# Transposing rows of q, k and the index query unsplit, two heads at once, and scoring each pair of heads on the two halves of the array's rows

## The chip, the cores and the metric

The kernel runs on one core of one Trainium2 chip. The metric is the device time of one execution in microseconds (us). Three runs of the kernel before took 591.34, 591.34 and 590.7 us, with a median of 591.34 us. The profile shown here belongs to one more execution, which took 590.16 us.

## The reference, cut to what matters

The program is one layer of a streaming encoder on 256 tokens of width 1024, in float32. An input projection yields, among other things, 16 query heads, 4 key and value heads, 8 heads of an index query with one shared index key (all of 64 elements), and the inputs of a state-space branch. The index scores choose 64 keys for every token, attention runs over the chosen keys, and the state-space branch runs beside it. Both branches are merged, and a mixture of 32 experts follows.

```
q  = rope(rmsnorm(q));  k = rope(rmsnorm(k));  iq = rope(iq);  ik = rope(rmsnorm(ik))
score[q,s]  = sum_h  iw[q,h] * relu(iq[q,h,:] . ik[s,:] / 8)         (8 index heads)
chosen[q]   = the 64 keys s with the largest score among the admissible ones
logit[h,q,s] = q[q,h,:] . k[s,h//4,:] / 8      for the chosen s      (16 heads)
o = softmax(logit) @ v
x = x + (sigmoid(ga) * (o @ W_a) + sigmoid(gb) * (ssd @ W_b)) @ W_out
x = x + experts(rmsnorm(x))
```

The part that the change touches is the way from the normalized rows of q, k, iq and ik to the two kinds of scores.

## The kernel before, in words

**Two parts per number.** Most matmuls run on operands of the type float32r, and a float32 value is kept as a rounded high part and a low part that holds the difference. A product of two such values takes three matmuls: high by high, high by low, low by high (`PASSES`). The weights come from memory as `w_raw` and are split into `w_hl`: ScalarE makes the high part (L174), and VectorE or GpSimd makes the low part (L178).

**Stages.** The tokens form two tiles of 128 (t = 0 and 1). The projections of q, k, the index query and the gates run as chunks of 512 columns (`wide_chunk`, L316), those of the state-space branch as chunks of 256 columns (`cm_chunk`, through `mm3`, L263). Beside these chunks runs a side stream, the generator `side()`, from which `interleave` takes a step between chunks: it handles the index key, the index query, the keys, the index scores, the queries and the attention. Later come the state-space groups, the branch projections (`ps_A`, `ps_S`), the output projection (`ps_o`), the routing, and eight rounds of four experts (`pgu`, `py`, `acc`) whose weights `we` stream in from memory on SyncE's queue, 96 tiles in a ring.

**The order of the work** is set by a planner, which simulates a timeline and gives each engine its list; each engine then goes through its list in order. Program order counts as priority, so a side step that is ready goes ahead of the chunk that follows it.

**From rows to scores.** `qk_tile` puts out the normalized and rotated rows `qn` of one token tile, 128 by heads by 64. `split_stack` (q and the index query, 8 heads at once) makes a tile `st` in which the high part (ScalarE, L389) and the low part (VectorE, L390) of each head lie side by side, 128 wide. `stack_T` transposes each head's 128 columns on TensorE against the identity (L379) and copies four heads at a time out of PSUM, on ScalarE (L382) for the first four, on VectorE (L384) for the others. So in `qT` and `iqT` a head's high part lies on partitions 0 to 63 and its low part on 64 to 127. `key_tile` does the same for keys, but stacks high on high and, in a second tile, low on low (L397, L399). A head's score then takes two matmuls over all 128 rows: the query's stack against the high keys, then against the low keys (L464 for the index, L541 in `attention`). 68 transposes, 32 matmuls of index scores and 64 of attention scores are issued in all.

**Buffers.** The pool `paux` in PSUM has two buffers with the tag "x" (transposes, `pt`, `po`) and two with the tag "s" (scores, a bank each). In `attention` one "s" buffer holds the scores of two heads; VectorE reads it with an instruction for each head (L545) that adds the bias and takes the maximum. In `index_proc` ScalarE reads it with one instruction (L467).

## Time and profile before

| quantity | value |
|---|---|
| median of three runs | 591.34 us |
| the profiled execution | 590.16 us |
| its span, from the first to the last instruction | 588.3 us |
| TensorE busy | 555.8 us, 94% of the span |
| VectorE busy | 332.1 us, 56% |
| ScalarE busy | 272.3 us, 46% |
| GpSimd busy | 240.0 us, 41% |
| memory read | 157.54 MB |

The busy share of TensorE is that of overlapping records: a matmul's record is longer than the time until the next one starts. The time that a run of equal matmuls takes is read from the start of the run to the start of the next one.

### The profile page before, as it was taken

The page shows a single profiled execution, that of the slowest core. Times are in us where ns is not written, and L with a number is a line of the kernel's source. Part 1 is how long each engine was busy: PE and PEld are TensorE (multiplying, and loading weights), DVE is VectorE, ACT ScalarE, POOL GpSimd, SP SyncE. Part 2 cuts the span into 40 slices and gives each one's busy share as a digit, 9 for nine tenths or more (in the row PEclk, how much of TensorE's full clock was granted, in tenths as well). Part 3 has the DMA queues.
Part 4 walks back from the last instruction along what each step waited for, and adds up shares of the span by engine and source line. Part 5 has one row for each costly group of instructions (what it writes and reads, how often), then busy time and mean ns, then how long its engine had stood idle before and what let it go on. Part 6 is the DMA issues. An engine that isn't in the chain of part 4 may idle for free.

```text
span 588.3 us, 9924 instructions
## 1 busy us (share of the span) xinstructions
PE 555.8 (94%) x3605; PEld 401.1 (68%) x3605; DVE 332.1 (56%) x711; ACT 272.3 (46%) x633; POOL 240.0 (41%) x250
## 2 busy tenths in 40 slices
PE   8999989999999999999999999999898898896996
PEld 5878768798898999889878888954354354241422
DVE  4669974999995888999594656551111212110101
ACT  7567567658897688877763535500000000000001
POOL 4677685666764376675767644100000000000000
PEclk9999999999999999999999999999999998987999
DMA  7755255353334595445766599989999999999994
GB/s 270 253 175 180 72 162 154 125 189 125 129 125 161 174 365 214 143 129 185 237 218 253 180 346 387 406 332 418 418 413 413 419 419 409 418 418 421 409 414 153
DMA packets 35811, 159.27 MB, mean 271 GB/s; under 512 B 4144, under 2 KB 5808, under 8 KB 27184
## 3 DMA queue, kind: packets, MB, share of 16 engines
q1 hardware_dynamic: 34464, 157.30, 71.2%
q10 hardware_dynamic: 1296, 1.30, 0.6%
q8 instruction: 30, 0.49, 0.3%
q14 instruction: 21, 0.17, 0.1%
HBM read 157.54 MB, written 1.05 MB: 270 GB/s over the span
## 4 chain that ended last, share of the span: by engine, by line
PE 63%; DMA 19%; DVE 8%; issue 3%; POOL 3%; ACT 2%; SPq 0%; ACTq 0%; DVEq 0%; POOLq 0%
DMA we<-wgu 13%; PE ps_xs L263 8%; PE ps_S L316 7%; PE ps_z L263 6%; PE ps_g L316 5%; PE pgu L1059 4%; DMA we<-wdn 4%; PE ps_A L316 4%; PE py L1119 3%; PE ps_g L1052 3%; PE acc L1134 2%; PE ps_o L316 2%; PE ps_k L316 2%; PE ps_iq L316 2%; PE ps_o L263 2%
## 5 line engine op out<-in xcount | busy, mean ns | idle before, releaser
L178 POOL TENSOR_TENSOR w_hl<-w_raw,w_hl 128x512 fp32r<-128x512 f32 (+1 forms) x101 | 140.7, 1396 | 87.8 <-ACT w_hl L174 70.1
L174 ACT CAST w_hl<-w_raw 128x512 fp32r<-128x512 f32 (+1 forms) x212 | 125.8, 620 | 47.7 <-PE ps_S L316 19.0
L178 DVE TENSOR_TENSOR w_hl<-w_raw,w_hl 128x512 fp32r<-128x512 f32 (+1 forms) x111 | 97.9, 889 | 36.6 <-ACT w_hl L174 36.0
L1059 PE MATMUL pgu<-we,xg 128*32 128x512 f32 x512 | 63.4, 603 | 4.6 <-DMA we<-wgu 4.6
L1077 POOL TENSOR_TENSOR dc<-Dm,cmr 128x128 f32<-128x128 f32 x16 | 6.1, 401 | 148.8 <-DVE Dm L982 133.5
L263 PE MATMUL ps_z<-hT,w_hl 128*128 128x256 f32 x384 | 51.6, 286 | 0.0
L263 PE MATMUL ps_xs<-hT,w_hl 128*128 128x256 f32 x384 | 50.7, 285 | 0.0
L263 PEld LDWEIGHTS ps_z<-hT,w_hl 128*128 128x128 f32 x384 | 47.7, 190 | 2.0 <-issue 1.8
L263 PEld LDWEIGHTS ps_xs<-hT,w_hl 128*128 128x128 f32 x384 | 47.5, 191 | 2.1 <-issue 2.1
L316 PE MATMUL ps_g<-w_hl,gT 128*128 128x512 f32 x192 | 47.8, 398 | 0.0
L316 PE MATMUL ps_S<-w_hl,yT 128*128 128x512 f32 x192 | 44.9, 392 | 0.0
L1055 DVE TENSOR_TENSOR xg<-ps_g,cmoe 128x512 f32<-128x512 f32 (+2 forms) x18 | 11.4, 631 | 56.8 <-PE ps_g L1052 56.7
L1059 PEld LDWEIGHTS pgu<-we,xg 128*32 128x32 f32 x512 | 15.4, 110 | 40.8 <-issue 25.9
L1052 PEld LDWEIGHTS ps_g<-Dm,x_sb 128*128 128x128 f32 x256 | 31.2, 191 | 16.5 <-issue 13.0
L316 PEld LDWEIGHTS ps_g<-w_hl,gT 128*128 128x128 f32 x192 | 35.1, 188 | 8.8 <-issue 0.8
L316 PEld LDWEIGHTS ps_S<-w_hl,yT 128*128 128x128 f32 x192 | 35.7, 188 | 7.6 <-issue 0.2
L1119 PE MATMUL py<-we,aTt 128*32 128x512 f32 (+1 forms) x272 | 35.7, 651 | 4.1 <-DVE aTt L1105 2.1
L1097 DVE SCALAR_TENSOR_TENSOR ac<-th,pgu 128x256 f32<-128x256 f32 x8 | 3.4, 421 | 60.6 <-ACT th L1095 60.6
L1130 ACT COPY y<-py 128x512 f32<-128x512 f32 (+1 forms) x9 | 4.8, 539 | 65.5 <-PE py L1119 65.5
L1052 PE MATMUL ps_g<-Dm,x_sb 128*128 128x128 f32 x256 | 33.5, 280 | 0.0
L1134 PE MATMUL acc<-y,dcT 128*128 128x512 f32 (+1 forms) x68 | 32.4, 604 | 0.9 <-DVE y L1132 0.8
L1095 ACT ACTIVATE th<-pgu,rs 128x256 f32<-128x256 f32 x8 | 3.8, 474 | 60.4 <-PE pgu L1059 60.4
(308 smaller groups left out, 977.0 us busy)
## 6 DMA issues: line engine op xcount, KB each, us to landing
we<-wgu SPq DMA_DIRECT2D x42, 1024.0 KB, 13.6
w_raw<-wwide SPq DMA_DIRECT2D x60, 512.0 KB, 3.7
we<-wdn SPq DMA_DIRECT2D x25, 1024.0 KB, 13.7
w_raw<-win SPq DMA_DIRECT2D x44, 512.0 KB, 3.8
we<-wgu SPq DMA_DIRECT2D x44, 512.0 KB, 10.3
we<-wdn SPq DMA_DIRECT2D x14, 512.0 KB, 10.2
x_sb<-xin SPq DMA_DIRECT2D x2, 512.0 KB, 4.4
w_raw<-wsm SPq DMA_DIRECT2D x1, 512.0 KB, 5.7
```

Source lines behind the costliest of these rows:

```text
L174: return act.copy(self.hl[i][:, 0], self.raw[i])
L178: return eng.tensor_sub(hl[:, 1], self.raw[i], hl[:, 0].bitcast(F32))
L263: pe.matmul(ps, lhsT=lhs[k][:, a], rhs=rhs[k][:, b], start=j == 0 and k == 0 and i == 0, stop=j == len(regions) - 1 and k == KD - 1 and i ...
L316: pe.matmul(ps[t], lhsT=lhs[t][k][:, a], rhs=w[k][:, b], start=k == 0 and i == 0, stop=k == KD - 1 and i == 2)
L1052: pe.matmul(ps[:, kk, :], lhsT=x1[:, t, (k + kk) * P:(k + kk + 1) * P], rhs=Dm[:, t].rearrange("p e j -> p (e j)"), start=t == 0, stop=t == 1)
L1055: dve.tensor_tensor(xg[:, ks, :], ps, fgain[:, ks].unsqueeze(2).to_broadcast([P, n, P]), op=ALU.mult)
L1059: i = pe.matmul(pgu[32 * e:32 * e + 32, :], lhsT=xg[:, k, 32 * e:32 * e + 32], rhs=wg[k][e], start=k == 0, stop=k == KD - 1, tile_position ...
L1077: pool.tensor_tensor(dc[:, t], Dm[:, t], cmr[:, t, 4 * q:4 * q + 4].unsqueeze(2).to_broadcast([P, 4, NSLOT]), op=ALU.mult)
L1095: act.activation(th, pgu[:, 0:256], AF.Tanh, scale=rs)
L1119: i_py = pe.matmul(py[32 * e:32 * e + 32, :], lhsT=aTt[:, f, 32 * e:32 * e + 32], rhs=wd[2 * n + f][e][:, c], start=f == 0, stop=f == 1, t ...
L1130: act.copy(y, py)
L1134: pe.matmul(acc[t][n][:, c], lhsT=dcT[:, t * P:(t + 1) * P], rhs=y, start=False, stop=q == 7 and c.stop == 512)
```

## The change

Four helpers are replaced. `heads_T` transposes the unsplit rows, two heads (128 columns) at once, so that one head of a pair lies on partitions 0 to 63 and the other on 64 to 127; the split into high and low part is made while the result is copied out of PSUM, by one instruction of ScalarE and one of VectorE. Keys and the index key are first doubled (`kd`, a copy on ScalarE) so that each key head lies on both halves. `pair_scores` then scores a pair of heads: three passes, and in each pass one matmul over rows 0 to 63 and one over rows 64 to 127, into two different "s" buffers. `index_proc` and `attention` take two "s" buffers at once, for four heads, where they took one at a time for two.

```
@@ -370,35 +370,27 @@
         pool.tensor_tensor(qn[:, :, 8:16], rc[:, :, 8:16], rs[:, :, 0:8], op=ALU.add)
         yield qn
 
-    def stack_T(dst, st, t, nh, name):
-
-        for h0 in range(0, nh, 4):
-            n = min(4, nh - h0)
-            ps = paux.tile([P, 4, P], F32, tag="x", name="psT_" + name)
-            for h in range(n):
-                pe.transpose(ps[:, h, :], st[:, h0 + h].rearrange("p a d -> p (a d)").bitcast(F32), ident)
-            o = dst[:, h0:h0 + n, t * P:(t + 1) * P]
-            if h0 == 0:
-                act.copy(o, ps[:, :n, :])
-            else:
-                dve.tensor_copy(o, ps[:, :n, :])
-
-    def split_stack(dst, qn, t, nh, name):
-
-        st = att.tile([P, 8, 2, HD], F32R, tag="st", name="st_" + name)[:, :nh]
-        act.copy(st[:, :, 0, :], qn)
-        dve.tensor_sub(st[:, :, 1, :], qn, st[:, :, 0, :].bitcast(F32))
-        stack_T(dst, st, t, nh, name)
-
-    def key_tile(dst_hi, dst_lo, qn, t, nh, name):
-        st = att.tile([P, 8, 2, HD], F32R, tag="st", name="st_" + name)
-        sth, stl = st[:, 0:nh], st[:, 4:4 + nh]
-        for a in range(2):
-            act.copy(sth[:, :, a, :], qn)
-        for a in range(2):
-            dve.tensor_sub(stl[:, :, a, :], qn, sth[:, :, 0, :].bitcast(F32))
-        stack_T(dst_hi, sth, t, nh, name + "h")
-        stack_T(dst_lo, stl, t, nh, name + "l")
+    def heads_T(dst, qn, t, n, name, twice=False):
+
+
+        ps = paux.tile([P, 4, P], F32, tag="x", name="psT_" + name)
+        if twice:
+            kd = att.tile([P, 4, 2, HD], F32, tag="kd", bufs=1, name="kd_" + name)[:, :n]
+            act.copy(kd, qn.unsqueeze(2).to_broadcast([P, n, 2, HD]))
+            qn = kd.rearrange("p h a d -> p (h a) d")
+        for i in range(n):
+            pe.transpose(ps[:, i, :], qn[:, 2 * i:2 * i + 2].rearrange("p a d -> p (a d)"), ident)
+        o = dst[:, :, :n, t * P:(t + 1) * P]
+        act.copy(o[:, 0], ps[:, :n, :])
+        dve.tensor_sub(o[:, 1], ps[:, :n, :], o[:, 0].bitcast(F32))
+
+    def pair_scores(q, k, i, tok, nk, out):
+
+
+        for n, (a, b) in enumerate(PASSES):
+            for r in range(2):
+                rows = slice(HD * r, HD * r + HD)
+                pe.matmul(out[r], lhsT=q[rows, a, i, tok], rhs=k[rows, b, :nk], start=n == 0, stop=n == 2)
 
     def interleave(chunks, side, per):
 
@@ -422,8 +414,8 @@
 
     iws = att1.tile([P, 2, 8], F32, name="iws")
     dtx = ssd1.tile([P, 2, 32], F32, name="dtx")
-    ikT = att1.tile([P, 2, T], F32R, name="ikT")
-    iqT = bigt([P, 8, T], F32R, "iqT")
+    ikT = att1.tile([P, 2, 1, T], F32R, name="ikT")
+    iqT = bigt([P, 2, 4, T], F32R, "iqT")
     v_sb = att1.tile([P, 2, 256], F32, name="v_sb")
 
     def first_chunk():
@@ -444,10 +436,10 @@
         for t in range(2):
             q = qk_tile(ps0[:, t, 0:64], t, 1, 2, "ik")
             next(q)
-            key_tile(ikT[:, 0:1, :], ikT[:, 1:2, :], next(q), t, 1, "ik")
+            heads_T(ikT, next(q), t, 1, "ik", twice=True)
 
     def iq_proc(q, t):
-        split_stack(iqT, next(q), t, 8, "iq")
+        heads_T(iqT, next(q), t, 4, "iq")
 
     iq_scale = 0.125 * 8
 
@@ -456,22 +448,21 @@
     def index_proc(t):
         nk = P * (t + 1)
         sc = att1.tile([P, nk], F32, name=f"sc{t}")
-        for hp in range(4):
-            ps = paux.tile([P, 2, T], F32, tag="s", name="ps_i")
-            for hh in range(2):
-                h = 2 * hp + hh
+        tok = slice(t * P, (t + 1) * P)
+        for p0 in range(0, 4, 2):
+            ps = [paux.tile([P, 2, T], F32, tag="s", name="ps_i") for _ in range(2)]
+            for i in range(2):
+                pair_scores(iqT, ikT[:, :, 0], p0 + i, tok, nk, [ps[r][:, i, :nk] for r in range(2)])
+            for r in range(2):
+                rel = att.tile([P, 2, T], F32, tag="sm", bufs=SMB, name="rel")[:, :, :nk]
+                act.activation(rel, ps[r][:, :, :nk], AF.Relu, scale=iq_scale)
                 for i in range(2):
-                    pe.matmul(ps[:, hh, :nk], lhsT=iqT[:, h, t * P:(t + 1) * P], rhs=ikT[:, i, :nk],
-                              start=i == 0, stop=i == 1)
-            rel = att.tile([P, 2, T], F32, tag="sm", bufs=SMB, name="rel")[:, :, :nk]
-            act.activation(rel, ps[:, :, :nk], AF.Relu, scale=iq_scale)
-            for hh in range(2):
-                h = 2 * hp + hh
-                if h == 0:
-                    dve.tensor_scalar(sc, rel[:, 0, :], iws[:, t, 0:1], None, op0=ALU.mult)
-                else:
-                    dve.scalar_tensor_tensor(sc, rel[:, hh, :], iws[:, t, h:h + 1], sc, op0=ALU.mult, op1=ALU.add)
-            yield
+                    h = 2 * (p0 + i) + r
+                    if h == 0:
+                        dve.tensor_scalar(sc, rel[:, 0, :], iws[:, t, 0:1], None, op0=ALU.mult)
+                    else:
+                        dve.scalar_tensor_tensor(sc, rel[:, i, :], iws[:, t, h:h + 1], sc, op0=ALU.mult, op1=ALU.add)
+                yield
         dve.memset(sc[0:64, nk - 64:nk], NEGI)
         dump(f"sc{t}", sc)
         for r in range(8):
@@ -490,15 +481,15 @@
     def k_proc(ps, t):
         if t == 0:
             kT.append(bigt([P, 2, 4, T], F32R, "kT"))
-        key_tile(kT[0][:, 0], kT[0][:, 1], next(ps), t, 4, "k")
+        heads_T(kT[0], next(ps), t, 4, "k", twice=True)
 
     def v_proc(ps, t):
         act.activation(v_sb[:, t], ps[t][:, 256:512], AF.Copy, scale=rx[:, t:t + 1])
 
     def q_proc(ps, c, t):
         if t == 0:
-            qT.append(bigt([P, 8, T], F32R, f"qT{c}"))
-        split_stack(qT[c], next(ps), t, 8, f"q{c}")
+            qT.append(bigt([P, 2, 4, T], F32R, f"qT{c}"))
+        heads_T(qT[c], next(ps), t, 4, f"q{c}")
 
     def h_part(k2):
 
@@ -527,22 +518,21 @@
 
     def attention(t, jp):
         nk = P * (t + 1)
+        tok = slice(t * P, (t + 1) * P)
         PTs = []
         for jj in range(2):
             j = 2 * jp + jj
             PT = [att.tile([P, 4, P], F32, tag=f"PT{kt}", name=f"PT{kt}") for kt in range(t + 1)]
             PTs.append(PT)
+            ps = [paux.tile([P, 2, T], F32, tag="s", name="ps_s") for _ in range(2)]
             for g2 in range(2):
-                ps = paux.tile([P, 2, T], F32, tag="s", name="ps_s")
-                for gg in range(2):
-                    h = 4 * j + 2 * g2 + gg
-                    q = qT[h // 8][:, h % 8, t * P:(t + 1) * P]
-                    for i in range(2):
-                        pe.matmul(ps[:, gg, :nk], lhsT=q, rhs=kT[0][:, i, j, :nk], start=i == 0, stop=i == 1)
+                p = 2 * j + g2
+                pair_scores(qT[p // 4], kT[0][:, :, j], p % 4, tok, nk, [ps[r][:, g2, :nk] for r in range(2)])
+            for g2 in range(2):
                 sm = att.tile([P, 2, T], F32, tag="sm", bufs=SMB, name="sm")[:, :, :nk]
                 mx = att.tile([P, 2], F32, tag="mx", name="mx")
                 for gg in range(2):
-                    dve.tensor_tensor_reduce(out=sm[:, gg, :], in0=ps[:, gg, :nk], in1=bias_t[t], scale=1.0,
+                    dve.tensor_tensor_reduce(out=sm[:, gg, :], in0=ps[gg][:, g2, :nk], in1=bias_t[t], scale=1.0,
                                              scalar=SENT, op0=ALU.add, op1=ALU.max, accum_out=mx[:, gg:gg + 1])
                 act.activation(mx, mx, AF.Copy, scale=-8.0)
                 su = att.tile([P, 2], F32, tag="su", name="su")
@@ -570,7 +560,6 @@
             late = po_half(1, kt)
             with tc.issue_after(late.ins):
                 po_half(0, kt)
-        tok = slice(t * P, (t + 1) * P)
         act.copy(aT[jp][:, 0, :, tok], po)
         dve.tensor_sub(aT[jp][:, 1, :, tok], po, aT[jp][:, 0, :, tok].bitcast(F32))
```

## Rows read from the trace of the kernel before

**Rows 1.** Busy time by stretch: us, time and instructions of each engine, clock, DMA.
```profile
28.00:185.00 157.00, 153.17 (x948) 131.62 (x948) 130.60 (x297) 111.74 (x284) 106.32 (x116) 1.00 0.45 146
185.00:330.00 145.00, 144.80 (x1010) 126.20 (x1007) 118.09 (x210) 104.00 (x221) 89.30 (x75) 1.00 0.60 208
...
443.00:588.00 145.00, 122.87 (x808) 50.83 (x804) 22.27 (x49) 9.56 (x20) 3.04 (x8) 0.93 0.96 390
```

**Rows 2.** The chain that ended last: start us, us, what.
```profile
409.38 1.72 PE acc L1134 x4
...
454.73 19.88 DMA we<-wgu
```

**Rows 3.** What TensorE waited for between 28 and 180 us: total, times, longest.
```profile
PE ps_q L316 <- POOL w_hl L178: 2.0, 2, 1.0
PE ps_s L541 <- DVE mx L545: 1.7, 3, 0.8
```

**Rows 4.** GpSimd in order of time: start us, us, what, idle time before.
```profile
58.82 1.29 POOL L506 TENSOR_TENSOR h<-gT 128x512 f32<-128x512 f32 x1 [4.23 <-DVE sc L473]
64.71 0.25 POOL L99 TENSOR_SCALAR ss_q<-ss_q 128x8 f32<-128x8 f32 x1 [4.59 <-DVE ss_q L355]
...
78.31 1.72 POOL L178 TENSOR_TENSOR w_hl<-w_raw,w_hl 128x512 fp32r<-128x512 f32 x1
```

**Rows 5.** TensorE in order of time, transposes and scores before.
```profile
89.21 1.03 PE L379 MATMUL psT_q<-ident,st_q 128*128 128x128 f32 x8
90.00 1.09 PE L541 MATMUL ps_s<-kT,qT 128*128 128x128 f32 x8
90.93 1.15 PE L316 MATMUL ps_q<-w_hl,gT 128*128 128x512 f32 x4
...
113.55 0.87 PE L541 MATMUL ps_s<-kT,qT 128*128 128x256 f32 x6
114.25 5.77 PE L316 MATMUL ps_g<-w_hl,gT 128*128 128x512 f32 x24
```

**Rows 6.** TensorE in order of time, a run on two column halves.
```profile
151.22 1.96 PE L263 MATMUL ps_xs<-hT,w_hl 128*128 128x256 f32 x15
153.10 1.94 PE L566 MATMUL po<-PT,v_sb 128*64 128x512 f32 x8
154.97 2.05 PE L263 MATMUL ps_xs<-hT,w_hl 128*128 128x256 f32 x15
156.86 0.60 PE L379 MATMUL psT_q<-ident,st_q 128*128 128x128 f32 x4
...
161.04 1.95 PE L263 MATMUL ps_xs<-hT,w_hl 128*128 128x256 f32 x15
162.83 0.38 PE L557 MATMUL pt<-ident,sm 128*128 128x128 f32 x2
```

**Rows 7.** Weight loads in order of time, at the same run on column halves.
```profile
153.10 0.20 PEld L566 LDWEIGHTS po<-PT,v_sb 128*64 128x64 f32 x4
```

**Rows 8.** Groups of weight loads over the span: count, busy us, mean ns, idle.
```profile
L541 PEld LDWEIGHTS ps_s<-kT,qT 128*128 128x128 f32 x64 | 8.6, 190 | 2.6 <-DVE mx L545 2.3
...
L566 PEld LDWEIGHTS po<-PT,v_sb 128*64 128x64 f32 x24 | 1.4, 135 | 1.9 <-issue 0.9 <-ACT st_q L389 0.3 <-ACT w_hl L174 0.3
```

**Rows 9.** Groups by form, 28 to 185 us: VectorE, then ScalarE; busy us, mean ns.
```profile
L390 DVE TENSOR_TENSOR st_q<-qn_q,st_q 128x512 fp32r<-128x512 f32 x4 | 4.7, 1180 | 4.1 <-ACT st_q L389 4.0
L384 DVE CAST qT<-psT_q 128x512 fp32r<-128x512 f32 x4 | 2.7, 683 | 0.0
L399 DVE TENSOR_TENSOR st_k<-qn_k,st_k 128x256 fp32r<-128x256 f32 x4 | 2.6, 687 | 0.0
L575 DVE TENSOR_TENSOR aT<-po,aT 128x512 fp32r<-128x512 f32 x3 | 2.0, 678 | 0.0
L390 DVE TENSOR_TENSOR st_iq<-qn_iq,st_iq 128x512 fp32r<-128x512 f32 x2 | 1.4, 682 | 0.0
...
L389 ACT CAST st_q<-qn_q 128x512 fp32r<-128x512 f32 x4 | 2.5, 622 | 7.5 <-POOL qn_q L370 7.5
```

## The prediction

> **What bounds the kernel now.** First the table of busy times by stretch [rows 1]. The change touches what runs between 28 and 185 us. There TensorE has records in 153.2 of 157 us at full granted clock (1.00), VectorE in 130.6, ScalarE in 111.7, GpSimd in 106.3, and the DMA share is 0.45. So TensorE bounds the stretch, VectorE is next, and the memory is idle half the time. From 185 to 330 us it is the same picture (144.8 of 145). After 443 us it turns round: the DMA share is 0.96 and TensorE has records in 122.9 of 145 us.
>
> Then the chain that ended last: from 454.7 us on it lies for 19.9 us at a stretch on the transfer of expert weights [rows 2]. That last part is bound by the stream of weights, but the stream can run at its full rate only once the buffers of the earlier stages come free, which TensorE decides. I therefore pass a microsecond saved or lost before 330 us one to one to the end. If it were hidden by the stream, the change would do nothing, and no row speaks for that.
>
> Then what TensorE waited for [rows 3]: only 2.0 us for low parts of weights from GpSimd, and 1.7 us for VectorE to give back a score buffer. That is all that relief of other engines can bring on TensorE's side. Last the cause of the 2.0 us [rows 4]: GpSimd waited 4.2 and 4.6 us for VectorE up to 64.7 us, then worked through a queue that ends with the late split at 78.3 us. So a VectorE that is some microseconds ahead by 64 us removes this wait.
>
> **The change part by part.** No DMA is added, removed or moved, and no queue of SyncE or GpSimd is passed. The terms are these.
>
> *Transposes.* Before there were 4 for the index key, 16 for k (high and low apart), 16 for the index query and 32 for q; each kind is halved, so of 68, 34 go. Eight take 0.79 us from the first to what follows, 0.10 us each [rows 5]. They stand in TensorE's list among chunk matmuls without a gap, so all of it counts: 34 x 0.10 = -3.4 us.
>
> *Scores, if the two halves run side by side.* Before, 96 matmuls; eight with 128 columns take 0.93 us and six with 256 take 0.70 us, so 0.117 us each at either width [rows 5], 11.2 us in all. After, 24 pairs (4 index, 8 attention, for each token tile) by 3 passes by 2 halves are 144 matmuls. Side by side they are 72 steps: 8.4 us, -2.8 us. One after the other they are 16.8 us, +5.6 us. No run on row halves stands in the trace; the nearest row is the run on column halves, where eight 512-column matmuls of full float32 that would take 0.43 us each on the whole array [rows 2] fit in 1.87 us between their start and that of the chunk after them [rows 6]. That is four steps, not eight, and in it four loads of half width, 0.135 us each by the mean [rows 8], all begin and end within 0.20 us [rows 7]. I take -2.8 us as likeliest and keep +5.6 us.
>
> *The toll of entering and leaving.* In the same stretch the two runs of 15 chunk matmuls and the eight on halves take 156.86 - 151.22 = 5.64 us [rows 6]. A chunk matmul of this width takes (162.83 - 161.04) / 15 = 0.119 us in an undisturbed run [rows 6]. So 5.64 - 30 x 0.119 - 4 x 0.43 = 0.35 us are spent on going over to halves and back. The load of the next weights, which otherwise hides under the matmul before it, stands bare on both sides. On row halves the first load has 128 columns instead of 64; by the mean records, 0.19 against 0.135 us [rows 8], that is 0.05 us more: 0.40 us for each visit. From below it is zero, if row halves need no such change; less than zero is excluded, since a change of layout removes no work. The present scores pay nothing: no idle time stands before them or behind them in [rows 5].
>
> The Trainium skill, TensorEngine Tiling (Array Packing), section "Key Properties", says that a change of the tiling mode, but not of the tile within a mode, drains TensorE; the trace agrees for column halves with the 0.35 us above, and no run here shows row halves. By that rule the forecast's sum holds, without it the sum of the second rival.
>
> *How many visits.* At least 12: the code asks for 12 matmuls at a time (two pairs), four such lots in the index and eight in the attention. At most 24 if the planner separates every pair, since transposes of softmax rows, which come earlier in the program, may break in. I take 15: 15 x 0.40 = +6.0 us; ends 12 x 0.40 = 4.8 and 24 x 0.40 = 9.6 us.
>
> *VectorE and ScalarE.* For q VectorE loses four low parts at 1.18 and four copies at 0.68 us, for the index query two low parts at 0.68 and two copies taken at the price of those for q, for the keys four low parts at 0.69 [rows 9]: 4.7 + 2.7 + 1.4 + 1.4 + 2.7 = 12.9 us. It gains eight subtractions out of PSUM; the same form stands in L575 at 0.68 us [rows 9], 5.4 us. So -7.5 us. ScalarE loses six casts at 0.62 us [rows 9] and about as much is left for the keys, where a doubling copy comes in: about -4 us. About 4 us of VectorE's part fall before 64 us, which is as much as the wait that started the chain in [rows 4]; I count the 2.0 us of TensorE's wait for GpSimd as gone, with 0 as the other end.
>
> *The score buffers.* Both "s" buffers are now taken at once and by four heads, so a lot of scores waits until VectorE has read all four heads of the lot before. Behind the waiting score on TensorE stand chunk matmuls, and VectorE waits for the scores. The same wait cost 1.7 us in three places [rows 3]. There are fewer but longer lots, and VectorE is less loaded, so I leave it at 1.7 us; the ends are 0 and, with a wait of 0.8 us at each of the six attention lots that follow another, 4.8 us, so -1.7 to +3.1 us.
>
> Sum: -3.4 - 2.8 + 6.0 - 2.0 = -2.2 us. The profiled execution took 590.16 us, 1.9 us of them outside its span, so its like would take 588.0 us; it lies 1.2 us below the median of 591.34 us, and from the median I get 589.1 us.
>
> **The rivals.**
>
> 1. *The planner tears the pairs apart: slower.* The two "s" buffers come free one after the other, since VectorE reads one head's bank and then the other's (ScalarE likewise in the index). The planner may place the matmuls of the first half as soon as the first buffer is free and let chunk matmuls in before the second half. Then there are 24 visits, 9.6 us, and half of the pairing is lost, (-2.8 + 5.6) / 2 = +1.4 us. Sum -3.4 + 1.4 + 9.6 - 2.0 = +5.6 us, 596.9 us. With pairing kept but 24 visits it is +1.4 us, 592.7 us. It decides from (3.4 + 2.8 + 2.0) / 0.40 = 20.5 visits on. For it: runs of scores before are mostly of four, as single buffers came free. Against it: the first lots after the keys and the queries find both buffers free.
>
> 2. *Row halves need no change of mode.* Then the toll is gone: -8.2 us, 583.1 us. Against it stands only the row of another kind of halves.
>
> 3. *The halves' loads take turns.* A step then costs two loads, and the scores +5.6 us: -3.4 + 5.6 + 6.0 - 2.0 = +6.2 us, 597.5 us. Against it: four loads of column halves run within 0.20 us [rows 7]. For it: with 128 columns the scores already take as long as with 256 [rows 5], so the load sets their pace. The Trainium skill, TensorE: Matmul & The Clock Gate, section "LDWEIGHTS", has the load's time go with its columns and not its rows, by which a half-row load is no shorter; the trace shows the columns' part (0.135 against 0.19 us, [rows 8]), and no run here shows the rows'.
>
> 4. *The waits for score buffers grow*, with 15 visits: -2.2 + 3.1 = +0.9 us, 592.2 us.
>
> **How the numbers follow.** The forecast has a chance of 0.42, with its own range from -5 us (12 visits, a shorter score wait) to 0 (the wait for GpSimd stays): 586.3 to 591.3 us. Rival 1 has 0.25, rival 2 0.15, rival 3 0.10, rival 4 0.08. A measurement of this kernel can tell about 0.2%, 1.2 us, from no change. Faster: 0.31 of the forecast and all of rival 2, 0.46. Within 0.2%: 0.09 of the forecast, 0.05 of rival 1, 0.04 of rival 4, 0.18. Slower: the rest, 0.36. The range leaves out the farther half of rival 2 and of rival 3 and the tail of rival 1: 583.5 to 596.5 us.
>
> **What would show it.** In the profile after: 34 transposes (`psT`) at 0.10 us; 144 score matmuls with 64 rows, their starts in pairs some ns apart (right) or 0.11 us apart (rival 3); bare time of about 0.2 us at either end of each run of them (right) or none (rival 2); 12 to 18 runs of them (right) or over 20 (rival 1); no wait of `ps_q` for GpSimd; the wait of `ps_s` for VectorE near 1.7 us (rival 4: 3 us or more). What would make it wrong altogether is a planner that, given other durations, orders the chunks and splits anew over the whole stretch, so that waits come up at places which this trace doesn't show.

## The result and the profile after

The kernel after took 595.86 us in the median of four executions (595.7 to 596.75), the kernel before 591.24 us on the same chip. The ratio is 1.0082 with a 95% interval of [1.0069, 1.0094]: the change costs 4.9 us. The forecast was 589.1 us, faster. The time lies inside the range of 583.5 to 596.5 us, but the sign was wrong. The profiled execution took 596.01 us, 594.2 us of them in its span (before: 590.16 and 588.3 us).

First the busy times by stretch of the kernel after, with the same columns as in [rows 1].

```profile
28.00:185.00 157.00, 151.76 (x910) 124.44 (x909) 122.10 (x282) 104.89 (x265) 104.03 (x114) 0.98 0.42 139
185.00:330.00 145.00, 144.96 (x1040) 128.13 (x1039) 120.36 (x210) 102.39 (x220) 86.53 (x74) 1.00 0.61 212
80.00:87.00 7.00, 6.92 (x21) 5.52 (x22) 2.69 (x4) 1.86 (x4) 5.34 (x9) 0.58 0.59 198
```

In this window VectorE fell from 130.6 to 122.1 us and ScalarE from 111.7 to 104.9 us. The window holds less of the program than before, so the change itself is better read from the groups of instructions that it replaces: on VectorE they went from 14.1 to 6.1 us, near the forecast's -7.5 us, and on ScalarE from 12.9 to 7.1 us. Over the whole span VectorE gained nothing by it, 332.6 us against 332.1 us, above all because the same 111 low parts of weights took longer. Before, then after:

```profile
L178 DVE TENSOR_TENSOR w_hl<-w_raw,w_hl 128x512 fp32r<-128x512 f32 (+1 forms) x111 | 97.9, 889 | 36.6 <-ACT w_hl L174 36.0
L178 DVE TENSOR_TENSOR w_hl<-w_raw,w_hl 128x512 fp32r<-128x512 f32 (+1 forms) x111 | 105.0, 955 | 40.7 <-ACT w_hl L174 40.2
```

TensorE, which bounds the stretch, got nothing for the relief either: fewer of its instructions fit into the same 157 us (910 against 948), and between 80 and 87 us its granted clock is 0.58 in the mean, between the two levels of 2.4 and 1.2 GHz. The kernel before had 1.00 there.

What TensorE waited for between 28 and 190 us after (total us, times, longest), which answers to [rows 3]:

```profile
PE ps_q L316 <- POOL w_hl L178: 3.5, 1, 3.5
PE ps_s L393 <- DVE mx L535: 0.7, 1, 0.7
```

The score buffers cost less than before (0.7 against 1.7 us). The wait for GpSimd, which was to go, grew from two of 1.0 us to one of 3.5 us. In TensorE's own order of time it looks like this (start us, us, what, and in brackets the idle time before it):

```profile
75.60 0.96 PE L316 MATMUL ps_q<-w_hl,gT 128*128 128x512 f32 x3
80.08 2.93 PE L316 MATMUL ps_q<-w_hl,gT 128*128 128x512 f32 x6 [3.52 <-POOL w_hl L178]
82.81 1.05 PE L382 MATMUL psT_q<-ident,qn_q 128*128 128x128 f32 x4
83.52 6.44 PE L316 MATMUL ps_q<-w_hl,gT 128*128 128x512 f32 x22
```

After the wait six chunk matmuls begin within 82.81 - 80.08 = 2.73 us, 0.45 us each, and the four transposes behind them 83.52 - 82.81 = 0.71 us, nearly 0.18 us each. Undisturbed it is 0.23 and 0.10 us. So time is lost twice here, once in standing still and once at the lower level of the clock.

The cause lies upstream, on VectorE and then GpSimd. VectorE, kernel after, in order of time:

```profile
58.65 1.86 DVE L464 SCALAR_TENSOR_TENSOR sc<-rel,iws,sc 128x128 f32<-128x128 f32 x2
60.58 0.11 DVE L466 MEMSET sc<- 64x64 f32 x1
...
66.23 0.29 DVE L470 MAX8 m<-sc 128x8 f32<-128x128 f32 x1
66.44 0.67 DVE L355 TENSOR_REDUCE ss_q<-sq_q 128x8 f32<-128x512 f32 x1
```

GpSimd, kernel after, which answers to [rows 4]:

```profile
63.80 1.30 POOL L178 TENSOR_TENSOR w_hl<-w_raw,w_hl 128x512 fp32r<-128x512 f32 x1 [3.83 <-ACT w_hl L174]
67.20 0.62 POOL L99 TENSOR_SCALAR ss_q<-ss_q 128x8 f32<-128x8 f32 x1 [2.09 <-DVE ss_q L355]
67.90 3.54 POOL L101 TENSOR_TENSOR ss_q<-ss_q,mhalf 128x8 f32<-128x8 f32 x1
...
76.69 2.11 POOL L101 TENSOR_TENSOR ss_q<-ss_q,mhalf 128x8 f32<-128x8 f32 x1
78.77 1.26 POOL L178 TENSOR_TENSOR w_hl<-w_raw,w_hl 128x512 fp32r<-128x512 f32 x1
```

The index scores of VectorE end at 60.7 us in either kernel. The planner, working with other costs, then put the sum of squares of q (L355) behind the eighth round of MAX8 instead of the fifth: it starts at 66.44 us instead of 63.95 us. GpSimd starts on it at 67.20 instead of 64.71 us [rows 4], and its power takes 3.54 us instead of 2.11 us. In the kernel before it was VectorE's sum, GpSimd's power, and the first of the two splits for which TensorE waited:

```profile
63.95 0.67 DVE L355 TENSOR_REDUCE ss_q<-sq_q 128x8 f32<-128x512 f32 x1
66.60 2.11 POOL L101 TENSOR_TENSOR ss_q<-ss_q,mhalf 128x8 f32<-128x8 f32 x1
76.05 1.29 POOL L178 TENSOR_TENSOR w_hl<-w_raw,w_hl 128x512 fp32r<-128x512 f32 x1
```

Now this split begins at 78.77 us, 2.7 us later (GpSimd has one split less to do in between), while TensorE reaches the place at 76.6 us, as before (76.4 us). The second split, that of 78.31 us in [rows 4], comes at 81.45 us after, but TensorE at half clock no longer notices.

Last the scores. TensorE, kernel after, a lot issued whole and one torn:

```profile
161.66 0.98 PE L393 MATMUL ps_s<-kT,qT 64*128 64x256 f32 x12
162.57 2.18 PE L263 MATMUL ps_xs<-hT,w_hl 128*128 128x256 f32 x16
...
165.97 0.97 PE L393 MATMUL ps_s<-kT,qT 64*128 64x256 f32 x6
166.87 0.62 PE L263 MATMUL ps_xs<-hT,w_hl 128*128 128x256 f32 x3
167.42 0.97 PE L393 MATMUL ps_s<-kT,qT 64*128 64x256 f32 x6
```

The weight loads (PEld) of the first and the second of these runs:

```profile
161.66 0.77 PEld L393 LDWEIGHTS ps_s<-kT,qT 64*128 64x128 f32 x12 [0.17 <-DVE acc L614]
165.97 0.77 PEld L393 LDWEIGHTS ps_s<-kT,qT 64*128 64x128 f32 x6
```

Twelve matmuls in pairs take 162.57 - 161.66 = 0.91 us, and six of one row half alone take 166.87 - 165.97 = 0.90 us. That is pairing in one line: six steps of 0.118 us in both cases, and 0.20 us for going over, about half of it in the first step and half in the last. It also shows how pairing is lost. One score buffer came free before the other, the planner issued the first half of four heads, let three chunk matmuls in, and came back for the second half.

**The account.** From the start times of all TensorE records up to the first matmul of the branch projection `ps_S`, each record is charged the time until the next one starts; what one of the 1440 chunk matmuls up to there takes beyond 0.232 us (512 columns) or 0.119 us (256) is a wait, the half clock, or the cost of going over to halves. The start of `ps_S` moved by 312.24 - 307.07 = +5.2 us:

| Part | before | after | difference | forecast |
|---|---|---|---|---|
| transposes (68, then 34) | 6.25 | 4.20 | -2.05 | -3.4 |
| score matmuls, leaving halves included | 11.57 | 14.52 | +2.95 | } -2.8 + 6.0 = +3.2 |
| entering halves, first matmul behind them (before: the column halves of `po` and `py`, which stay) | 3.4 | 5.8 | +2.4 | } |
| waits and half clock | 6.4 | 9.2 | +2.8 | -2.0 |
| all else | | | -0.9 | 0 |

There were 20 visits to row halves, not 15. At 0.20 us each they hold 4.0 of the 14.52 us, and 0.3 us more are waits of transposes behind the first index scores, so the steps themselves took 10.2 us against 11.57 us: pairing was worth some 1.4 us instead of 2.8 us. Of 72 pairs, 47 start within 15 ns of each other; others run out of phase and overlap in part, and 12 matmuls of the two torn runs shown don't overlap at all. The visits cost 4.0 + 2.4 = 6.4 us in this account, 0.32 us each. That is the least: 16 of their 40 ends lie at transposes and `po`, and what is lost there is charged to these. Between chunk matmuls the two torn runs above give the whole price: 166.87 - 165.97 - 6 x 0.118 = 0.19 us within a run and 167.42 - 166.87 - 3 x 0.119 = 0.19 us on the chunk matmuls behind and ahead, 0.39 us unrounded.

### The profile page after: what moved, and what is told of

Its sections match the earlier page's. It is cut to its first block, busy times and chain, and to the rows that moved or that the text cites. A ratio compares the mean times of both kernels' runs of the same rounds, so it can differ in the third digit from the quotient of the medians.

```text
span 594.2 us, 9922 instructions
## 1 busy us (share of the span) xinstructions
PE 560.6 (94%) x3619; PEld 401.3 (68%) x3619; DVE 332.6 (56%) x701; ACT 268.5 (45%) x619; POOL 238.5 (40%) x250
## 4 chain that ended last, share of the span: by engine, by line
PE 60%; DMA 20%; DVE 9%; POOL 5%; ACT 3%; issue 3%; ACTq 0%; POOLq 0%; SPq 0%; DVEq 0%
DMA we<-wgu 11%; PE ps_z L263 8%; PE ps_xs L263 8%; PE ps_S L316 7%; DMA we<-wdn 7%; PE pgu L1048 4%; PE ps_A L316 4%; PE ps_g L1041 3%; PE py L1108 3%; PE acc L1123 2%; PE ps_q L316 2%; DVE w_hl L178 2%; PE ps_o L316 2%; PE ps_g L316 2%; DMA w_raw<-wwide 2%
## 5 line engine op out<-in xcount | busy, mean ns | idle before, releaser
L178 DVE TENSOR_TENSOR w_hl<-w_raw,w_hl 128x512 fp32r<-128x512 f32 (+1 forms) x111 | 105.0, 955 | 40.7 <-ACT w_hl L174 40.2
L263 PE MATMUL ps_xs<-hT,w_hl 128*128 128x256 f32 x384 | 52.0, 287 | 0.0
## 6 DMA issues: line engine op xcount, KB each, us to landing
we<-wdn SPq DMA_DIRECT2D x14, 512.0 KB, 10.2
```

The costliest lines, as they stand in the source:

```text
L178: return eng.tensor_sub(hl[:, 1], self.raw[i], hl[:, 0].bitcast(F32))
L263: pe.matmul(ps, lhsT=lhs[k][:, a], rhs=rhs[k][:, b], start=j == 0 and k == 0 and i == 0, stop=j == len(regions) - 1 and k == KD - 1 and i ...
```

## The experiments

Two theories were set against each other. V: the visits to row halves, with torn pairs, are the loss. W: the wait before the second q chunk, with the clock behind it, is the loss. From run 9 on the expectations call V with the torn pairs "theory T". Each ratio is to the kernel before on the same chip.

**Run 1: one low part less for GpSimd, in the kernel after.**

```diff
-FEW = (2, 3, 5)
+FEW = (2, 3, 5, 6)
```

> The changed kernel, with one low part of four instead of two given to GpSimd in the chunk of the second half of q (FEW gets a 6). Theory W (the wait): most of the loss of 4.6 us is the 3.5 us that TensorE waits at 76 us for a low part from GpSimd, and the 6.8 us at half clock behind it; with the part on VectorE the wait shrinks below 1 us, the clock stays at 1.00, and the time falls by 3 to 5 us, to 591 to 593 us. Theory V (the visits): the loss is the price of going over to row halves, 19 runs at 0.40 us against gains of 6.2 us in transposes and pairing, and the wait is paid back later; then the time stays at 595 to 596 us.

Measured: 594.25 us, ratio 1.0054 [1.0036, 1.0072], between the two. The wait fell from 3.5 to 1.0 us, but another of 1.0 us came up for the rotated q of GpSimd just ahead of it, and the clock (third column from the end) fell all the same:

```profile
80.00:90.00 10.00, 8.99 (x43) 6.90 (x44) 5.58 (x14) 3.08 (x6) 4.65 (x6) 0.83 0.36 115
```

That alone decides nothing, and the next run shows one more reason.

**Run 2: the same setting in the kernel before.** The edit is that of run 1.

> The kernel before, with the same setting of FEW. Theory W: its two waits of 1.2 us at the same place go, 589 to 590 us. Theory V: waits there are paid back later, 591 us.

Measured: 594.98 us, ratio 1.0057 [1.0037, 1.0077]. Both theories missed. TensorE's waits up to 190 us are no longer than before:

```profile
PE ps_s L541 <- DVE mx L545: 1.1, 1, 1.1
PE ps_q L316 <- POOL w_hl L178: 0.9, 1, 0.9
```

Yet the start of `ps_S` moved from 307.1 to 310.1 us, with new waits of 2.1 us at 192 us (`ps_c`) and 1.6 us at 249 us (`ps_xs`). So the setting itself costs 3.4 us in a kernel that doesn't need it, and with it the two kernels are equal (1.0057 and 1.0054). Within the same setting nothing of the change's loss is left; that speaks for W, or for a rearrangement as large as either cause.

**Run 3: scores on the whole rows.** The transposes stay unsplit, but each head's score is two matmuls over all 128 rows, so 96 as before, and no row halves. The scores are then not those of the reference.

```diff
-        for n, (a, b) in enumerate(PASSES):
+        for n in range(2):
             for r in range(2):
-                rows = slice(HD * r, HD * r + HD)
-                pe.matmul(out[r], lhsT=q[rows, a, i, tok], rhs=k[rows, b, :nk], start=n == 0, stop=n == 2)
+                pe.matmul(out[r], lhsT=q[:, r, i, tok], rhs=k[:, n, :nk], start=n == 0, stop=n == 1)
```

> The changed kernel, scoring over all 128 rows of the array with two passes (96 matmuls, as before): the unsplit transposes alone, without row halves; its scores mix the two heads of a pair and aren't the reference's. Both theories: 19 visits at 0.40 us go (-7.6 us) and the pairing goes (+2.8 us). Theory V: 591 us or a little less. Theory W: the same if the wait at 76 us stays, 587 to 588 us if the planner's new order removes it; the profile tells which.

Measured: 588.59 us, ratio 0.9958 [0.9943, 0.9973]. That is 1.2% or 7.3 us less than the kernel after. In TensorE's order of time, the same place of the program:

```profile
159.57 0.64 PE L392 MATMUL ps_s<-kT,qT 128*128 128x256 f32 x4
160.05 0.88 PE L263 MATMUL ps_xs<-hT,w_hl 128*128 128x256 f32 x6
160.77 0.64 PE L392 MATMUL ps_s<-kT,qT 128*128 128x256 f32 x4
```

Four take 160.05 - 159.57 = 0.48 us, 0.12 us each, and nothing is lost on either side. In the account above, scores and the going over fall from 20.3 to 15.5 us, 4.8 of the 6.9 us by which `ps_S` starts earlier; 4.8 us is also what the visits less the pairing were to give. W alone can't be right, since TensorE's wait is still there in this run:

```profile
PE ps_q L316 <- POOL w_hl L178: 2.8, 1, 2.8
```

So V holds for the larger part, and the rest of the change, without row halves, is a gain of 2.5 us. The time itself is lower than the 591 us that both theories gave for a wait that stays; where the other 2 us come from, this run doesn't tell.

**Run 4: more visits.** A matmul on the whole array with 32 columns, unread, between the two pairs of each lot, the order tied.

```diff
+        if i % 2 == 0:
+            with tc.issue_after(last_s[0].ins):
+                last_s[0] = pe.matmul(ps_v, lhsT=q[:, 0, i, tok], rhs=k[:, 0, :32], start=True, stop=True)
```

> The changed kernel with one whole-array matmul of 32 columns put between the two pairs of each lot, tied in order: 12 more visits. If a visit costs 0.40 us on the path that sets the end: 12 x (0.40 + 0.11) = +6 us, 602 us. If visits are hidden in other waits: under +2 us, 596 to 598 us.

Measured: 600.35 us, ratio 1.0164 [1.0146, 1.0181], 4.9 us over the kernel after, with 34 visits instead of 20. TensorE in order of time:

```profile
160.51 0.62 PE L399 MATMUL ps_s<-kT,qT 64*128 64x256 f32 x6
161.06 0.28 PE L404 MATMUL ps_v<-kT,qT 128*128 128x32 f32 x1
161.28 0.62 PE L399 MATMUL ps_s<-kT,qT 64*128 64x256 f32 x6
161.83 1.93 PE L263 MATMUL ps_xs<-hT,w_hl 128*128 128x256 f32 x14
```

Six matmuls in pairs take 161.83 - 161.28 = 0.55 us: three steps of 0.118 us and 0.20 us. Beside the 0.90 us of six unpaired ones in the kernel after, this prices pairing by itself: (0.90 - 0.55) / 3 = 0.117 us for each pair. This lot with its added visit takes 161.83 - 160.51 = 1.32 us, against 0.91 us for the whole lot of the kernel after: 0.41 us for the visit, its small matmul included. In the account the 14 added visits cost 4.7 us. So V's price of a visit is borne out. That the whole came out near it, at +4.9 us, is luck: the wait at 76 us shrank to 0.8 us, `ps_S` starts at 311.85 us, 0.4 us earlier than in the kernel after, and other time was lost behind that.

**Run 5: TensorE kept busy at the wait.** Eight unread matmuls, 1.9 us in sum, are put where TensorE would stand still.

```diff
+                if name == "q1" and (t, k, i) == (0, 1, 0):
+                    busy = paux.tile([P, 512], F32, tag="n", bufs=1, name="busy")
+                    with tc.issue_after(m.ins):
+                        for _ in range(8):
+                            pe.matmul(busy, lhsT=lhs[0][0][:, 0], rhs=w[0][:, 0], start=True, stop=True)
```

> The changed kernel with eight matmuls whose results nobody reads, 0.23 us each, put on TensorE where it waits 3.5 us for GpSimd's low part at 76 us. They fill 1.9 us of that wait and take nothing else. If the half clock behind the wait is a loss of its own: the clock stays at 1.00 there, the 12 matmuls that took 0.43 us each take 0.23, and the time falls by 2 to 2.4 us, to 593.5 us. If the clock falls all the same, or the gain is paid back: 595.9 us.

Measured: 593.81 us, ratio 1.0043 [1.0028, 1.0059], about 2.3 us less than the kernel after (0.0039 of 591). The busy times by stretch, clock in the third column from the end:

```profile
76.00:80.00 4.00, 3.74 (x17) 2.66 (x15) 2.36 (x4) 3.78 (x7) 3.93 (x4) 1.00 0.43 135
80.00:84.00 4.00, 2.84 (x12) 1.82 (x13) 2.45 (x3) 0.59 (x1) 4.00 (x5) 1.00 0.41 130
```

The clock stays at its upper level, where the kernel after had 0.58. More work on the bound engine made the kernel faster, which speaks for the half clock as a loss of its own, apart from the wait. It doesn't prove the size. `ps_S` starts 4.3 us earlier (307.91 us), but in the new order 55 pairs start together instead of 47, and scores with the going over cost 1.2 us less; against that stands a clock of 0.72 between 46 and 52 us, where the kernel after had 1.00. And part of the gain is lost again behind 330 us, where TensorE now waits for VectorE among the `ps_S` matmuls, as in no row of the kernel after.

```profile
337.32 3.01 PE L316 MATMUL ps_S<-w_hl,yT 128*128 128x512 f32 x12 [1.43 <-DVE w_hl L178]
```

**Run 6: only the keys unsplit.** The kernel before with the unsplit transposes for k and the index key alone, whose two halves are copies of one head; q, the index query and the scores stay as they were.

```diff
-            key_tile(ikT[:, 0:1, :], ikT[:, 1:2, :], next(q), t, 1, "ik")
+            heads_T(ikT, next(q), t, 1, "ik", twice=True)
-        key_tile(kT[0][:, 0], kT[0][:, 1], next(ps), t, 4, "k")
+        heads_T(kT[0], next(ps), t, 4, "k", twice=True)
```

> The kernel before with one part of the change alone: keys and the index key are doubled, transposed unsplit and split out of PSUM; queries are stacked and scored on whole rows as before, so there is no visit to row halves. 10 transposes less at 0.10 us (-1.0 us), 3.4 us less work on VectorE and ScalarE, and VectorE's list has the sum of squares of q ahead of the fifth of the eight rounds of the index choice, where the changed kernel has it behind the seventh. If the visits and the late order are what costs in the change, this is faster than before by 1 to 3 us: 588 to 590 us. If the doubling copy or the order of high part, low part out of PSUM costs, it is slower than 591 us.

Measured: 589.64 us, ratio 0.9977 [0.9966, 0.9988], faster than both kernels. Ten transposes go (58 remain), and TensorE's two largest waits are those of [rows 3]:

```profile
PE ps_q L316 <- POOL w_hl L178: 1.7, 2, 1.0
PE ps_s L555 <- DVE mx L559: 1.7, 3, 0.9
```

The sum of squares of q stands ahead of the fifth round here and starts at 63.22 us. The transposes took 5.59 instead of 6.25 us, `ps_S` starts 0.8 us earlier, and the time is 1.4 us lower (0.7 to 2.0), so where the sum of squares stayed early, the saving arrived.

**Run 7: one row half after the other.** The order of the loops in `pair_scores` is swapped, so that the three passes of one head come before those of the other.

```diff
-        for n, (a, b) in enumerate(PASSES):
-            for r in range(2):
+        for r in range(2):
+            for n, (a, b) in enumerate(PASSES):
```

> The changed kernel with the three passes of one half put ahead of the three of the other, so that fewer of a lot's 12 matmuls meet side by side: 9 steps for 6, by queue order, 12 lots by 3 steps by 0.117 us = +4.2 us. If pairing is worth what the sum of the prediction takes for it: 599 to 600 us. If pairing is worth little, since loads or reads of PSUM set the pace: 596 us.

Measured: 597.58 us, ratio 1.0130 [1.0114, 1.0147], 2.8 us over the kernel after. The direction is that of pairing being worth something, but the size isn't clean: the planner still brought some 40 pairs together (47 before the swap). In the profiled execution, the fastest of six at 595.89 us, the score matmuls took 1.0 us more, but `ps_S` starts 2.5 us earlier than in the kernel after; what makes the median longer isn't in its rows.

**Run 8: GpSimd made late in the kernel before,** by a second power, unread, for each tile of the first q chunk.

```diff
+            if kind == 0 and name == "q0":
+                r2 = att.tile([P, 8], F32, tag="ss2", bufs=1, name="late")[:, :nh]
+                pool.tensor_tensor(r2, r, mhalf.to_broadcast([P, nh]), op=ALU.pow)
```

> The kernel before with one more power of 2.1 us on GpSimd for each token tile of the first half of q, results unread, ahead of the late parts at 76 us: the wait that the changed kernel shows, without row halves. If a wait there goes through to the end (theory W): TensorE waits some 3 to 5 us there, the clock falls, and the time rises by 3 to 5 us, to 594 to 596 us. If waits there are paid back later: within 1 us of 591 us.

Measured: 589.76 us, ratio 0.9986 [0.9973, 0.9998]. The run failed as a test: the planner arranged the work anew, and TensorE's wait for GpSimd fell to a single 1.0 us instead of growing. It says nothing on W. It does say that work added to an engine can leave the time as it is: GpSimd's busy time between 28 and 185 us rose from 106.3 to 112.5 us.

**Run 9: both score buffers as one tile,** so that they come free together. The same tile serves the state-space products, which also took turns between the two buffers.

```diff
-            ps = [paux.tile([P, 2, T], F32, tag="s", name="ps_s") for _ in range(2)]
+            ps2 = paux.tile([P, 2, 2, T], F32, tag="s2", bufs=1, name="ps_s")
+            ps = [ps2[:, 0], ps2[:, 1]]
```

> The kernel after, with the two score buffers of a lot taken as one tile, so that both come free at the same time. Theory T (part of the pairing was lost because the buffers come free one after the other: in the kernel after only 47 of the 72 pairs of half-row matmuls start together): nearly all pairs start together, the visits stay about 20 (other work still breaks in between pairs), so 72 to 80 steps instead of 97 and, with the staggered steps of the kernel after that overlap anyway, 1 to 2 us less up to the state-space stage; against that stands a longer wait for the last head of the lot before. 594 to 596 us. If pairing is worth nothing: the same time as the kernel after, or more by the wait.

Measured: 607.86 us, ratio 1.0278 [1.0253, 1.0302]. As a version it is bad, for the state-space products now wait:

```profile
PE ps_b L744 <- ACT e L746: 2.9, 3, 1.3
PE py L764 <- DVE e L749: 1.6, 1, 1.6
```

Its scores can still be read: 67 of 72 pairs start together, with 20 visits as before, and the score matmuls take 13.93 instead of 14.52 us. Waits of transposes behind them are in both numbers, 1.18 and 0.34 us; without them it is 12.75 against 14.18 us. So the buffers' coming free in turn was what tore the pairs, and the tearing itself lost 1.4 us, within the 1 to 2 us expected.

**Run 10: lots issued whole,** by a higher priority in the planner for the score matmuls of the kernel after.

```diff
+                with tc.high_priority(100):
+                    pe.matmul(out[r], lhsT=q[rows, a, i, tok], rhs=k[rows, b, :nk], start=n == 0, stop=n == 2)
```

> The kernel after, with a higher priority for the score matmuls in the planner, so that a lot of 12 is issued whole: 13 visits to row halves instead of 20, all pairs together. Theory T (visits and torn pairs are what the change lost): 7 x 0.32 us of tolls and 1.8 us of pairing less, 4 us, about 592 us, if the wait for GpSimd before the second q chunk and the half clock behind it stay as in the kernel after. Theory W (the wait and its half clock are most of the loss): no more than 1 or 2 us less, 594 to 595 us.

Measured: 597.75 us, ratio 1.0108 [1.0085, 1.0132]; the interval overlaps that of the kernel after. There are 13 visits, 60 of 72 pairs start together, and scores with the going over cost 2.6 us less in the account (17.7 against 20.3), transposes 0.5 us less. At `ps_S` 1.6 us of it are left, at the end nothing. The wait at 76 us stays (2.8 us), and TensorE runs into a new one. TensorE, then VectorE, then GpSimd of this run, in order of time:

```profile
186.83 0.76 PE L263 MATMUL ps_xs<-hT,w_hl 128*128 128x256 f32 x5
189.80 0.38 PE L667 MATMUL ps_c<-prep,cprep 128*128 128x32 f32 x2 [2.21 <-issue]
```

```profile
185.91 0.22 DVE L659 TENSOR_TENSOR prep<-prep 128x64 f32<-128x64 f32 x1
186.09 0.69 DVE L178 TENSOR_TENSOR w_hl<-w_raw,w_hl 128x512 fp32r<-128x512 f32 x1
186.69 1.33 DVE L660 TENSOR_TENSOR prep<-prep 128x64 f32<-128x64 f32 x1
188.06 1.28 DVE L661 SCALAR_TENSOR_TENSOR prep<-dtx,prep 128x64 f32<-128x64 f32 x1
189.37 0.20 DVE L662 TENSOR_SCALAR dtx<-prep 128x64 f32<-128x64 f32 x1
189.48 0.22 DVE L664 SCALAR_TENSOR_TENSOR prep<-prep 128x64 f32<-128x64 f32 x1
```

```profile
186.65 2.61 POOL L178 TENSOR_TENSOR w_hl<-w_raw,w_hl 128x512 fp32r<-128x512 f32 x2 [3.12 <-ACT w_hl L174]
```

TensorE, ahead by now, reaches `ps_c` at 187.6 us, while VectorE is still in the chain of small steps that yields its operand. Two of these steps take 1.33 and 1.28 us instead of 0.2 us, for just as long as GpSimd works beside them. Behind the wait the clock is at 0.66 between 190 and 195 us. The 4 us of theory T were not seen at the end, though the visits came as said and most of the pairs did.

**Run 11: run 10 with the eight unread matmuls of run 5.**

> The same with eight unread matmuls at the wait for GpSimd in the second q chunk, as in the run that kept TensorE busy there. If the half clock behind the wait is a loss of its own, 2 us less than without them: about 590 us by T, 592 to 593 us by W. If the wait has moved elsewhere in the new order, the eight matmuls cost up to their own 1.9 us instead.

Measured: 596.88 us, ratio 1.0114 [1.0085, 1.0144]. The executions spread from 594.75 to 599.83 us. In the profiled one, of 595.21 us, `ps_S` starts 2.5 us earlier than in the kernel after, the wait for GpSimd is 1.0 us, and the clock is 1.00 throughout from 28 to 330 us, behind the wait for `ps_c` too:

```profile
187.00:190.00 3.00, 2.04 (x17) 2.07 (x18) 2.44 (x8) 1.18 (x5) 0.00 (x0) 1.00 0.78 232
190.00:196.00 6.00, 6.00 (x49) 5.89 (x48) 2.51 (x6) 2.44 (x5) 2.58 (x2) 1.00 0.57 180
```

At the end little of it is left; among the `ps_S` matmuls stands a wait for VectorE of 1.5 us, like that of run 5, and `ps_c` again costs 2.2 us. So a kernel without the half clock and with 13 visits is no faster than the kernel after: neither theory, nor their sum, gives this time.

## Why the prediction was wrong, point by point

**What bounds the kernel** held: TensorE bounds the stretch. But "a microsecond saved or lost before 330 us one to one to the end" failed as a rule for savings. Runs 6 and 3 passed on what they had saved at `ps_S`; runs 5, 10 and 11 didn't. There TensorE, which comes earlier, meets producers that are not ready (`ps_c` up to 2.2 us, `ps_S` 1.4 to 1.5 us).

**The relief of VectorE** is the step that failed. Its own size was right, 8.0 us of VectorE's work gone against 7.5 us forecast. Wrong was that "a VectorE that is some microseconds ahead by 64 us removes this wait". VectorE was not ahead at 60.7 us, for the index scores end at the same time; up to 66 us it had waited 6.3 us for ScalarE's casts of weights, against 4.4 us before. Then the planner's new order put the sum of squares 2.5 us later, and with it the split for which TensorE waits. The term of -2.0 us became +2.8 us, a miss of 4.8 us, which is more than all others together. The +2.8 us are 1.5 us of longer wait and some 2.4 us of half clock, which was not in the list at all, less the 1.0 us that the score buffers gave back. That the wait starts with the later sum of squares is read from the two traces, and no run has undone it alone. It isn't enough by itself: in run 4 the sum starts as late (66.46 us), but the power takes 2.19 us, TensorE comes to the place later, and its wait is 0.8 us.

**The scores.** Side by side was right: matmuls of the two halves start 1 to 13 ns apart, and rival 3 falls. The mechanism of the toll was right too, and rival 2 falls: 0.40 us forecast, 0.39 us between chunk matmuls, 0.41 us with its small matmul in run 4, at least 0.32 us in the mean of the kernel after. Mis-sized were the visits (20 for 15) and the pairing (-1.4 for -2.8 us), together +5.3 for +3.2 us. This is rival 1 in part. It was to decide from 20.5 visits; at the 20 found, tolls of 6.4 us stand against 3.5 us from transposes and pairing, and the 2.0 us of relief that were to make up most of the rest didn't come. The Trainium skill, TensorEngine Tiling (Array Packing), section "Key Properties", says that tiles load weights and multiply independently and that changing the mode drains TensorE; the two rows of twelve and of six matmuls agree with the first, the 0.39 us lost around and in each of the two torn runs with the second.

**The transposes** gave -2.05 instead of -3.4 us. The 34 left took 4.20 us, 0.12 us each against 0.09 us for the 68 before. Four of them fell into the half clock (0.71 us instead of 0.4 us), and behind four others a visit to row halves followed at once, which put 0.1 us of entering on each of these.

**The score buffers** were counted at no change and gave 1.0 us back (0.7 for 1.7 us); rival 4 falls.

**What would make it wrong altogether** was named: a planner that orders chunks and splits anew. That is what happened, and it had no chance of its own in the sum. That the time of 595.86 us still lies inside the stated range is luck: the range was drawn around the rivals, and none of them holds what happened at the wait.

**What stays open.** Row halves against whole rows is a difference of 7.3 us between two runs on the chip (run 3), and the price of a visit is shown in rows (0.39 us, run 4). That the half clock behind the wait costs 2.3 us of the end time (run 5) is likely and not shown, since run 11 lost it without a gain. The two don't add up to a loss of 4.9 us with the gain of the transposes; each edit moves the planner's order and with it waits of 1 to 4 us, in the kernel before as well (run 2). What the wait alone costs, at full clock, is not settled: runs 1, 2 and 8, which were to show it, moved other work. Runs 10 and 11 show that fewer visits alone don't bring the time back, but not which of the new waits would have to go for it. So the 4.9 us are not divided up among their causes.

## What to carry to other kernels

Before short runs of matmuls are put on parts of the array, count how often TensorE will go over to that mode, from the number of places where other work can break in and not from the lots in the code; here 20 visits cost at least 6.4 us and the pairing brought 1.4. Relief of an engine that is not the bound is worth something only if what the bound engine waits for starts earlier, so follow that one chain in the trace and don't count busy time. Where a planner orders the work, test each part of a change alone: the part that left the sum of squares early (run 6) kept its gain.

## What the runs showed of the hardware

**Halves of the rows.** Twelve loads of 64 rows and 128 columns in pairs take the same 0.77 us as six on one half alone, and in the runs shown a pair of matmuls of 256 columns takes the same 0.118 us as one. A visit to the halves between chunk matmuls costs 0.39 us.

**The clock after a wait.** A wait of 3.5 us was followed by a granted clock of 0.58 from 80 to 87 us, one of 2.2 us in run 10 by 0.66 over 5 us. Two waits of 1.0 us, 0.7 us apart, were followed by 0.83 over 10 us in run 1. But two waits of 1.0 us in the kernel before, one of 2.1 us in run 2 (at 192 us) and one of 2.2 us in run 11 left it at 1.00, so in these runs the length of the wait alone doesn't tell. With eight unread matmuls in the wait at 76 us the clock stayed at 1.00 (runs 5 and 11).

**VectorE beside GpSimd.** Two steps of VectorE on 128x64 elements took 1.33 and 1.28 us while a split ran on GpSimd, and 0.22 and 0.23 us in the kernel after, where GpSimd stood idle. The Trainium skill, SBUF — State Buffer, section "SBUF: two separate sides", has VectorE, with two operands in SBUF, and GpSimd take turns on one pair of ports for whole instructions; the rows of these two steps agree. GpSimd's power took 3.54 us in the kernel after, with three splits of VectorE in its time, and 2.11 us in the kernel before, also with splits of VectorE beside it, so its length isn't explained here. In a dense schedule the duration of a small step thus depended on what the planner had put beside it.
